# The factors of 17 norms: one power on POOL instead of twelve steps on VectorE

## The chip, the cores and the metric

The kernel runs on one core of a Trainium2 chip. The metric is device time in microseconds (us) for one execution. Engines are named as the profile names them: PE is TensorE's matmuls (PEld its weight loads), DVE is VectorE, ACT is ScalarE, POOL is GpSimd, SP is the queue that issues the plain loads and stores.

## What is computed

One layer of a decoder: 512 tokens of width 1024, three attention branches side by side, then an expert layer. Nearly every operand is normalised by its root mean square, and these norms are what the change touches:

```
def rmsnorm(x, g):                      # over 1024 columns
    y = xf * lax.rsqrt(jnp.mean(xf * xf, axis=-1, keepdims=True) + EPS)
    return (y * g).astype(x.dtype)

def head_rmsnorm(x, g):                 # over the 64 or 128 columns of a head
    return xf * lax.rsqrt(jnp.mean(xf * xf, axis=-1, keepdims=True) + EPS) * g

h = rmsnorm(x, norm1_g);  z = h @ w_in                     # queries, keys, values, gates
fq, fk, sq, sk, mq, mk = head_rmsnorm(each, its gain)      # forgetting, window, memory attention
x = x + merged @ w_out                                     # three gated branches
x = x + peer_ffn(rmsnorm(x, norm2_g), ...)                 # 8 heads, 16 of 16384 experts each
```

So a norm needs, per token (and head), one factor: (mean square + 1e-6) to the power -0.5.

## The kernel before

The 512 tokens are four blocks of 128, one token per partition. Block 0 goes first and alone through the attention branches (`mixers(0)`), the three others follow together (`mixers(1)`). Beside `mixers(1)` runs the expert work of block 0: a search for its best keys, then a long chain of gathered expert rows. For each of its 128 chosen experts POOL issues an indirect DMA of 128 rows (L828, tile `row`, five buffers), and VectorE multiplies and sums them (L838, tile `scr`, for the first table; L844, tile `mg`, for the second). After the mixers comes the search for the other three blocks on VectorE (L681 to L685), then the dense part, in which blocks 2 and 3 run against all experts as matmuls while block 1's rows are gathered; that lasts from about 858 us to the end.

Matrix products are made from three matmuls on a weight split in two parts: ScalarE rounds the raw weight into `whi` (L107), and VectorE, for some weights POOL, subtracts it from the raw one into `wlo` (L119, L117). Up to the search, a scheduler puts the instructions of each engine in an order of its own by modelled times; from the dense part on the order is that of the code. Each engine works its queue strictly in that order.

A norm has three parts. The sums of squares come from ScalarE and a sum on VectorE (`rss` for whole rows, `hss` for heads). Then `rsqrt_mean` makes the factors, at most 24 columns in one call: L183 forms `rsv` = mean + epsilon; L184 and L185 shift its bits and subtract them from a constant, which is a first guess for the result (`rsy`); L187 to L189, three times, are Newton steps through `rsa`. All twelve run on VectorE. Then the factors are used: for a whole row as a scaled identity `dg` (L209, ScalarE) with which TensorE transposes and scales at once (L222); for heads as a scaling of `qn`, on VectorE for blocks 0 and memory (L324), on ScalarE for three blocks together (L328, one instruction for each head and block), after which TensorE transposes them (L342). `rstd` (L853, L935) keeps the factors of the second norm.

There are 17 such calls, with 1 to 24 columns and 138 in all; 13 come before about 300 us, four beside the gathers or at the search (342, 431, 535 and 703 us).

Of the kernel before, what the change touches and what calls it, by code (L numbers as in the profile page):

```python
# [7 lines left out]
F32 = mybir.dt.float32  # L8
F32R = mybir.dt.float32r
BF16 = mybir.dt.bfloat16  # L10
I32 = mybir.dt.int32
U32 = mybir.dt.uint32
AF = mybir.ActivationFunctionType
OP = mybir.AluOpType
# [34 lines left out]
def tile_block(ctx: ExitStack, tc: tile.TileContext, t: dict, out: bass.AP):  # L49
    nc = tc.nc  # L50
    V, A, PE, G = nc.vector, nc.scalar, nc.tensor, nc.gpsimd

    consts = ctx.enter_context(tc.tile_pool(name="consts", bufs=1))
    big = ctx.enter_context(tc.tile_pool(name="big", bufs=1))
    small = ctx.enter_context(tc.tile_pool(name="small", bufs=4))
# [112 lines left out]

    eps = consts.tile([128, 24], F32, name="eps")
    V.memset(eps, EPS)  # L170
    magic = consts.tile([128, 24], F32, name="magic")
    V.memset(magic, float(0x5F3759DF))
    ones_i = consts.tile([128, 24], I32, name="ones_i")
    V.memset(ones_i, 1)

    def rsqrt_mean(ss, n, size):

        v = small.tile([128, 24], F32, tag="rsv", name="rsv")
        sh = small.tile([128, 24], I32, tag="rsi", name="rsi", bufs=2)
        y = small.tile([128, 24], F32, tag="rsy", name="rsy")  # L180
        a = small.tile([128, 24], F32, tag="rsa", name="rsa")
        v, sh, y, a, n = v[:, :n], sh[:, :n], y[:, :n], a[:, :n], slice(0, n)
        V.scalar_tensor_tensor(v, ss, 1.0 / size, eps[:, n], op0=OP.mult, op1=OP.add)  # L183
        V.tensor_tensor(sh, v.bitcast(I32), ones_i[:, n], op=OP.logical_shift_right)  # L184
        V.scalar_tensor_tensor(y.bitcast(I32), sh, -1.0, magic[:, n], op0=OP.mult, op1=OP.add)  # L185
        for _ in range(3):
            V.tensor_mul(a, y, y)  # L187
            V.scalar_tensor_tensor(a, a, -0.5, v, op0=OP.mult, op1=OP.mult)
            V.scalar_tensor_tensor(y, a, 1.5, y, op0=OP.add, op1=OP.mult)  # L189
        return y  # L190

    def squares(x, dst):
# [7 lines left out]
    def factors(sums, nb):  # L200

        ss = small_f(BIG, "rss", 2)[:, :nb]
        V.reduce_sum(ss, sums[:, :nb], axis=AX.X)
        return rsqrt_mean(ss, nb, D)
# [88 lines left out]
    class Heads:  # L293
# [25 lines left out]
        def scale(self):  # L319
            r = rsqrt_mean(self.ss[:, :self.cols], self.cols, self.parts[0][3])  # L320
            for z, c, nh, hd in self.parts:
                for b in range(self.nb):
                    if self.nb < BIG:
                        V.tensor_mul(z[:, b, :, :hd], z[:, b, :, :hd],  # L324
                                     r[:, c + b * nh:c + b * nh + nh, None].to_broadcast([128, nh, hd]))
                        continue
                    for h in range(nh):
                        A.activation(z[:, b, h, :hd], z[:, b, h, :hd], AF.Copy,  # L328
                                     scale=r[:, c + b * nh + h:c + b * nh + h + 1])
# [857 lines left out]
```

## Time and profile before

| | us |
|---|---|
| median of 3 runs | 1792.46 (1791.27 to 1794.70) |
| the profiled execution | 1789.02 |
| its span, first to last instruction | 1786.5 |
| busy: PE / PEld | 1646.6 / 1367.5 |
| busy: DVE | 1349.1 |
| busy: ACT | 629.5 |
| busy: POOL | 812.9 |
| mean granted TensorE clock, share of full speed | 0.954 |

The busy time of an engine is a sum over stages with different limits, so a stage is read by itself. In a row of the timeline the bracket at the end tells how long that engine had been idle and what ended the idle time. PE's busy time includes overlap of one matmul with the next.

### The profile page before, as it was taken

How to read it: one execution, taken by the hardware profiler on the slowest of the kernel's cores; microseconds unless marked ns; L12 is line 12 of the kernel's file. 1: busy time of each engine (PE TensorE's matmuls, PEld its weight loads, DVE VectorE, ACT ScalarE, POOL GpSimd, SP SyncE). 2: the span in 40 equal slices, each digit the busy share in tenths (PEclk: the TensorE clock that was granted, in tenths of full speed). 3: DMA queues.
4: the chain of work that ended last, by engine and by line, in shares of the span. 5: the costliest groups of instructions: out<-in, count | busy, mean ns of one | idle time of the engine just before them, and what ended most of it. 6: DMA issues, size and time to landing. Idle time of an engine off the chain costs nothing.

```text
span 1786.5 us, 24816 instructions
## 1 busy us (share of the span) xinstructions
PE 1646.6 (92%) x8590; PEld 1367.5 (77%) x8590; DVE 1349.1 (76%) x2717; ACT 629.5 (35%) x1416; POOL 812.9 (45%) x719
## 2 busy tenths in 40 slices
PE   6899788999999989888899979989898999999998
PEld 5898777898987989877789967767666676666664
DVE  5787647969996999999989955656566676676765
ACT  5786545564544434221136631111111111111111
POOL 1000353646553558884068853434444444444542
PEclk8998989999996999989999999999999999999998
DMA  6786455969995899785389997989899999999996
GB/s 248 224 266 188 149 146 167 329 246 327 354 322 175 313 320 330 244 276 176 142 302 401 415 398 278 387 315 391 316 384 348 368 386 376 368 381 375 391 352 217
DMA packets 216813, 540.13 MB, mean 302 GB/s; under 512 B 17008, under 2 KB 95088, under 8 KB 216688
## 3 DMA queue, kind: packets, MB, share of 16 engines
q1 hardware_dynamic: 142960, 270.09, 43.0%
q0 software_dynamic: 73728, 268.47, 41.2%
q8 instruction: 67, 1.10, 0.2%
q14 instruction: 58, 0.48, 0.1%
HBM read 519.61 MB, written 18.87 MB: 301 GB/s over the span
## 4 chain that ended last, share of the span: by engine, by line
issue 33%; DVE 13%; DMA 13%; PE 12%; POOL 12%; ACT 1%; POOLq 0%; DVEq 0%; ACTq 0%
POOL row L828 11%; DMA row<-in_peer_v_dram,eidx 7%; DMA row<-in_peer_u_dram,eidx 6%; PE mm L918 5%; DVE mg L844 4%; DVE scr L838 1%; PE mm L132 1%; PE mm L133 1%; PE mm L131 1%; DVE tmp L683 1%; PE sc L989 1%; PE tp L989 1%; DVE wlo L119 1%; PE sc L496 1%; DVE ids L682 1%
## 5 line engine op out<-in xcount | busy, mean ns | idle before, releaser
L828 POOL DMA_INDIRECT row<-in_peer_u_dram,eidx x256 | 316.7, 1237 | 387.6 <-DVE scr L838 274.8
L918 PE MATMUL mm<-h2f,two 128*128 128x256 f32 x1920 | 442.8, 382 | 16.0 <-DMA two<-in_uT_dram 10.9
L828 POOL DMA_INDIRECT row<-in_peer_v_dram,eidx x256 | 312.0, 1219 | 282.9 <-DVE mg L844 207.9
L918 PEld LDWEIGHTS mm<-h2f,two 128*128 128x128 f32 x1920 | 363.4, 192 | 82.0 <-issue 27.8
L119 DVE TENSOR_TENSOR wlo<-raw,whi 128x1024 fp32r<-128x1024 f32 (+1 forms) x201 | 245.4, 1223 | 212.9 <-ACT whi L107 209.3
L844 DVE SCALAR_TENSOR_TENSOR mg<-row,acts,mg 128x1024 f32<-128x1024 f32 x256 | 356.4, 1392 | 24.2 <-DMA row<-in_peer_v_dram,eidx 21.6
L107 ACT CAST whi<-raw 128x1024 fp32r<-128x1024 f32 (+1 forms) x236 | 246.8, 1048 | 308.7 <-DMA raw<-in_peer_v_dram 182.4
L838 DVE SCALAR_TENSOR_TENSOR scr<-row,h2n 128x1024 bf16<-128x1024 f32 x256 | 313.3, 1224 | 35.1 <-DMA row<-in_peer_u_dram,eidx 30.1
L117 POOL TENSOR_TENSOR wlo<-raw,whi 128x1024 fp32r<-128x1024 f32 (+1 forms) x35 | 83.8, 2401 | 216.8 <-ACT whi L107 216.6
L922 ACT ACTIVATE ga<-mm 128x256 f32<-128x256 f32 x128 | 49.3, 386 | 374.1 <-PE mm L918 367.4
L131 PE MATMUL mm<-whi,hhi 128*128 128x256 f32 (+1 forms) x576 | 169.0, 295 | 5.3 <-ACT hhi L633 1.9
L132 PE MATMUL mm<-wlo,hhi 128*128 128x256 f32 (+1 forms) x576 | 166.6, 290 | 2.0 <-DVE wlo L119 2.0
L133 PE MATMUL mm<-whi,hlo 128*128 128x256 f32 (+1 forms) x576 | 166.0, 290 | 2.3 <-DVE hlo L634 1.1
L1030 PE MATMUL sc<-raw,ah 128*128 128x512 f32 x256 | 121.0, 595 | 0.8 <-DVE ah L1012 0.8
L1030 PE MATMUL tp<-raw,ah 128*128 128x512 f32 x256 | 120.3, 592 | 0.0
L131 PEld LDWEIGHTS mm<-whi,hhi 128*128 128x128 f32 x576 | 111.2, 194 | 8.5 <-ACT hhi L633 2.2
L132 PEld LDWEIGHTS mm<-wlo,hhi 128*128 128x128 f32 x576 | 111.3, 193 | 5.2 <-DVE wlo L119 2.9
L133 PEld LDWEIGHTS mm<-whi,hlo 128*128 128x128 f32 x576 | 111.2, 194 | 4.4 <-DVE hlo L634 1.4
L133 PE MATMUL mm<-hhi,wlo 128*128 128x384 f32 x320 | 110.8, 346 | 3.7 <-POOL wlo L117 3.7
L131 PE MATMUL mm<-hhi,whi 128*128 128x384 f32 x320 | 111.1, 347 | 1.5 <-ACT hhi L223 1.1
L132 PE MATMUL mm<-hlo,whi 128*128 128x384 f32 x320 | 112.1, 350 | 0.0
L1030 PEld LDWEIGHTS tp<-raw,ah 128*128 128x128 f32 x256 | 48.6, 190 | 61.2 <-issue 61.2
(265 smaller groups left out, 2834.6 us busy)
## 6 DMA issues: line engine op xcount, KB each, us to landing
raw<-in_peer_v_dram SPq DMA_DIRECT2D x128, 512.0 KB
two<-in_uT_dram SPq DMA_DIRECT2D x60, 1024.0 KB
raw<-in_w_nat_dram SPq DMA_DIRECT2D x40, 512.0 KB
gd<-st SPq DMA_DIRECT2D x32, 512.0 KB
gq<-gd SPq DMA_DIRECT2D x32, 512.0 KB
raw<-in_w_tr_dram SPq DMA_DIRECT2D x48, 256.0 KB
raw<-in_w_o_dram SPq DMA_DIRECT2D x24, 512.0 KB
raw<-in_w_tr_dram SPq DMA_DIRECT2D x24, 512.0 KB
```

The lines of the kernel that those rows point to most:

```text
L107: A.copy(hi[:, :n * w], raw[:, :n * w])
L117: G.tensor_tensor(lo, raw, hi.bitcast(F32), op=OP.subtract)
L119: V.tensor_sub(lo, raw, hi.bitcast(F32))
L131: PE.matmul(ps, lh, rh, start=first, stop=False)
L132: PE.matmul(ps, lh, rl, start=False, stop=False)
L133: PE.matmul(ps, ll, rh, start=False, stop=last)
L828: G.indirect_dma_start(out=r, out_offset=None, in_=t["peer_" + tab], in_offset=bass.IndirectOffsetOnAxis(ap=eidx[b][:, j:j + 1], axis=0))
L838: V.scalar_tensor_tensor(scr, r, 1.0, h2n[b], op0=OP.mult, op1=OP.mult, accum_out=acts[b][:, c]))
L844: V.scalar_tensor_tensor(x1[b], r, acts[b][:, c], x1[b], op0=OP.mult, op1=OP.add))
L918: PE.matmul(ps[:, :TD], w[:, dc], h2f[dc], start=dc == 0, stop=dc == KC - 1)
L922: A.activation(ga[k], ps[:, :TD], AF.Gelu)
L1030: PE.matmul(acc[i, hf], al[:, tok], w[0][:, d], start=k == 0, stop=k == NK - 1)
```

## The change

`rsqrt_mean` keeps its first step on VectorE (mean plus epsilon) and gets the factors by one two-input instruction on POOL, a power with a tile of -0.5 as exponent. The shift, the subtraction and the nine Newton steps go, with their constants and two work tiles. Nothing else in the code differs; the scheduler orders all instructions anew.

```
--- before.py
+++ after.py
@@ -168,25 +168,15 @@
 
     eps = consts.tile([128, 24], F32, name="eps")
     V.memset(eps, EPS)
-    magic = consts.tile([128, 24], F32, name="magic")
-    V.memset(magic, float(0x5F3759DF))
-    ones_i = consts.tile([128, 24], I32, name="ones_i")
-    V.memset(ones_i, 1)
+    mhalf = consts.tile([128, 24], F32, name="mhalf")
+    V.memset(mhalf, -0.5)
 
     def rsqrt_mean(ss, n, size):
 
-        v = small.tile([128, 24], F32, tag="rsv", name="rsv")
-        sh = small.tile([128, 24], I32, tag="rsi", name="rsi", bufs=2)
-        y = small.tile([128, 24], F32, tag="rsy", name="rsy")
-        a = small.tile([128, 24], F32, tag="rsa", name="rsa")
-        v, sh, y, a, n = v[:, :n], sh[:, :n], y[:, :n], a[:, :n], slice(0, n)
-        V.scalar_tensor_tensor(v, ss, 1.0 / size, eps[:, n], op0=OP.mult, op1=OP.add)
-        V.tensor_tensor(sh, v.bitcast(I32), ones_i[:, n], op=OP.logical_shift_right)
-        V.scalar_tensor_tensor(y.bitcast(I32), sh, -1.0, magic[:, n], op0=OP.mult, op1=OP.add)
-        for _ in range(3):
-            V.tensor_mul(a, y, y)
-            V.scalar_tensor_tensor(a, a, -0.5, v, op0=OP.mult, op1=OP.mult)
-            V.scalar_tensor_tensor(y, a, 1.5, y, op0=OP.add, op1=OP.mult)
+        v = small.tile([128, 24], F32, tag="rsv", name="rsv")[:, :n]
+        y = small.tile([128, 24], F32, tag="rsy", name="rsy")[:, :n]
+        V.scalar_tensor_tensor(v, ss, 1.0 / size, eps[:, :n], op0=OP.mult, op1=OP.add)
+        G.tensor_tensor(y, v, mhalf[:, :n], op=OP.pow)
         return y
 
     def squares(x, dst):
```

Three places show how the order moves. The first is ScalarE's queue at the start: the first norm's `dg` (L209, in the changed code L199) and the casts `whi` of the first weights. Before:

```order
L246 ACTIVATE gcol<-gcol 128x1
L209 ACTIVATE dg<-cst,rsy 128x128
L107 CAST whi<-raw 128x1056
L223 ACTIVATE hhi<-tp,gcol 128x128
L107 CAST whi<-raw 128x1056
L223 ACTIVATE hhi<-sc,gcol 128x128
L223 ACTIVATE hhi<-tp,gcol 128x128
L223 ACTIVATE hhi<-sc,gcol 128x128
```

In the changed kernel:

```order
L236 ACTIVATE gcol<-gcol 128x1
L107 CAST whi<-raw 128x1056 x2
L199 ACTIVATE dg<-cst,rsy 128x128
L185 ACTIVATE junk,sums<-mg_247 128x1024
L213 ACTIVATE hhi<-tp,gcol 128x128
L213 ACTIVATE hhi<-sc,gcol 128x128
L185 ACTIVATE junk,sums<-mg_247 128x1024
L213 ACTIVATE hhi<-tp,gcol 128x128
```

`dg` now stands behind both casts instead of ahead of them.

The second is VectorE's queue at the norm of the first forgetting-attention heads (66 us in the trace), eight factors for queries and keys. Before, from the last sum of squares:

```order
L310 TENSOR_REDUCE hss<-sq 128x4
L119 TENSOR_TENSOR wlo<-raw,whi 128x1024
L183 SCALAR_TENSOR_TENSOR rsv<-hss,eps 128x8
L119 TENSOR_TENSOR wlo<-raw,whi 128x1024
L184 TENSOR_TENSOR rsi<-rsv,ones_i 128x8
L185 SCALAR_TENSOR_TENSOR rsy<-rsi,magic 128x8
L119 TENSOR_TENSOR wlo<-raw,whi 128x1024
L187 TENSOR_TENSOR rsa<-rsy 128x8
L119 TENSOR_TENSOR wlo<-raw,whi 128x1024
L188 SCALAR_TENSOR_TENSOR rsa<-rsa,rsv 128x8
L119 TENSOR_TENSOR wlo<-raw,whi 128x1024
L189 SCALAR_TENSOR_TENSOR rsy<-rsa,rsy 128x8
```

In the changed kernel (L178 is the step that was L183, and L314 the scaling of `qn` that was L324):

```order
L119 TENSOR_TENSOR wlo<-raw,whi 128x1024 x2
L300 TENSOR_REDUCE hss<-sq 128x4
L119 TENSOR_TENSOR wlo<-raw,whi 128x1024
L178 SCALAR_TENSOR_TENSOR rsv<-hss,eps 128x8
L119 TENSOR_TENSOR wlo<-raw,whi 128x1024 x2
L314 TENSOR_TENSOR qn<-qn,rsy 128x4x64 x2
L119 TENSOR_TENSOR wlo<-raw,whi 128x1024 x2
```

The eleven steps and the weight splits between them are gone from between the first step and the scaling; two splits are left there.

The third is POOL's queue at the gathers for block 0 (`eidx` holds the chosen experts). Before:

```order
L696 TENSOR_TENSOR cand<-v_3471 128x16
L828 DMA row<-in_peer_u_dram,eidx_187 128x1024 x128
L828 DMA row<-in_peer_v_dram,eidx_187 128x1024 x32
L117 TENSOR_TENSOR wlo<-raw,whi 128x1024
L828 DMA row<-in_peer_v_dram,eidx_187 128x1024 x4
```

In the changed kernel (L179 is the power, L818 the gather):

```order
L686 TENSOR_TENSOR cand<-v_3325 128x16
L179 TENSOR_TENSOR rsy<-rsv,mhalf 128x24
L818 DMA row<-in_peer_u_dram,eidx_173 128x1024 x16
L179 TENSOR_TENSOR rsy<-rsv,mhalf 128x24
L818 DMA row<-in_peer_u_dram,eidx_173 128x1024 x35
L179 TENSOR_TENSOR rsy<-rsv,mhalf 128x24
L818 DMA row<-in_peer_u_dram,eidx_173 128x1024 x56
L179 TENSOR_TENSOR rsy<-rsv,mhalf 128x12
L818 DMA row<-in_peer_u_dram,eidx_173 128x1024 x21
L818 DMA row<-in_peer_v_dram,eidx_173 128x1024 x35
L117 TENSOR_TENSOR wlo<-raw,whi 128x1024
```

Four powers now stand in this queue ahead of and between the gathers; one more stands further on, behind 42 gathers of the second table.

## Rows read from the trace of the kernel before

**Rows 1.** Busy us by stage: length, PE, PEld, DVE, ACT, POOL, clock, DMA share, GB/s
```profile
0.00:290.00 290.00, 245.87 (x1785) 232.09 (x1785) 194.41 (x591) 185.47 (x377) 55.42 (x63) 0.92 0.65 202
...
290.00:700.00 410.00, 388.26 (x2464) 354.86 (x2465) 355.10 (x640) 194.16 (x464) 216.49 (x168) 0.93 0.84 294
...
700.00:858.00 158.00, 134.92 (x706) 125.12 (x704) 155.07 (x630) 37.40 (x71) 108.08 (x149) 0.94 0.69 227
```

**Rows 2.** Groups by line, the removed steps: count, busy us, mean ns, idle us
```profile
L189 DVE SCALAR_TENSOR_TENSOR rsy<-rsa,rsy 128x4 f32<-128x4 f32 (+7 forms) x51 | 13.2, 266 | 0.7
...
L187 DVE TENSOR_TENSOR rsa<-rsy 128x4 f32<-128x4 f32 (+7 forms) x51 | 10.3, 209 | 0.7
...
L188 DVE SCALAR_TENSOR_TENSOR rsa<-rsa,rsv 128x4 f32<-128x4 f32 (+7 forms) x51 | 7.8, 161 | 0.6
...
L185 DVE SCALAR_TENSOR_TENSOR rsy<-rsi,magic 128x4 int32<-128x4 int32 (+7 forms) x17 | 4.7, 287 | 0.2
...
L184 DVE TENSOR_TENSOR rsi<-rsv,ones_i 128x4 int32<-128x4 int32 (+7 forms) x17 | 4.7, 286 | 0.2
```

**Rows 3.** The timeline, norms at 296 and 431 us: start, us, engine, line
```profile
295.67 0.17 DVE L183 SCALAR_TENSOR_TENSOR rsv<-hss,eps 128x24 f32<-128x24 f32 x1
...
306.25 0.18 DVE L189 SCALAR_TENSOR_TENSOR rsy<-rsa,rsy 128x24 f32<-128x24 f32 x1
...
306.46 3.69 ACT L328 ACTIVATE qn<-qn,rsy 128x64 f32<-128x64 f32 x15 [7.38 <-DVE rsy L189]
...
306.87 0.42 PE L342 MATMUL tg<-cst,qn 128*66 128x128 f32 x1 [3.44 <-ACT qn L328]
...
312.82 0.85 PE L342 MATMUL tg<-cst,qn 128*66 128x128 f32 x3 [2.90 <-ACT kT L343]
...
430.70 0.18 DVE L183 SCALAR_TENSOR_TENSOR rsv<-hss,eps 128x24 f32<-128x24 f32 x1
...
451.17 0.17 DVE L189 SCALAR_TENSOR_TENSOR rsy<-rsa,rsy 128x24 f32<-128x24 f32 x1
```

**Rows 4.** The groups by line and shape on POOL, whole span
```profile
L828 POOL DMA_INDIRECT row<-in_peer_u_dram,eidx x256 | 316.7, 1237 | 387.6 <-DVE scr L838 274.8 <-issue 39.8 <-ACT qn L328 23.1
...
L117 POOL TENSOR_TENSOR wlo<-raw,whi 128x1024 fp32r<-128x1024 f32 x34 | 81.3, 2400 | 216.8 <-ACT whi L107 216.6
...
L696 POOL TENSOR_TENSOR cand<-v 128x24 f32<-128x24 f32 x32 | 9.3, 306 | 12.5 <-DVE tmp L683 6.5 <-DVE v L681 3.7 <-DVE best L681 2.2
```

**Rows 5.** The timeline of the first three norms
```profile
4.79 4.72 POOL L265 TENSOR_SCALAR slope<-cst 128x128 bf16<-128x128 f32 x8 [4.35 <-DMA cst<-in_c_mats_dram]
...
8.60 0.40 ACT L209 ACTIVATE dg<-cst,rsy 128x128 f32<-128x128 f32 x1 [2.32 <-DVE rsy L189]
...
10.70 1.07 ACT L107 CAST whi<-raw 128x1056 fp32r<-128x1056 f32 x1 [0.45 <-DMA raw<-in_w_skvf_dram]
...
24.04 0.48 PE L342 MATMUL tg<-cst,qn 128*128 128x128 f32 x1 [5.47 <-DVE qn L324]
```

**Rows 6.** The timeline of the norms at 66 and 243 us
```profile
66.17 0.16 DVE L183 SCALAR_TENSOR_TENSOR rsv<-hss,eps 128x8 f32<-128x8 f32 x1
...
75.17 0.17 DVE L189 SCALAR_TENSOR_TENSOR rsy<-rsa,rsy 128x8 f32<-128x8 f32 x1
...
75.95 0.60 PE L342 MATMUL tg<-cst,qn 128*66 128x128 f32 x4 [3.83 <-DVE qn L324]
...
251.45 1.43 PE L342 MATMUL tg<-cst,qn 128*128 128x128 f32 x3 [3.09 <-ACT qn L328]
```

**Rows 7.** The timeline of the last norm
```profile
707.81 2.96 DVE L189 SCALAR_TENSOR_TENSOR rsy<-rsa,rsy 128x3 f32<-128x3 f32 x1
...
708.33 2.41 POOL L117 TENSOR_TENSOR wlo<-raw,whi 128x1024 fp32r<-128x1024 f32 x1
...
718.27 2.62 DVE L189 SCALAR_TENSOR_TENSOR rsy<-rsa,rsy 128x3 f32<-128x3 f32 x1
...
722.85 2.08 PE L222 MATMUL tp<-dg,mg 128*128 128x128 f32 x8 [5.00 <-ACT dg L209]
```

## The prediction

> **What bounds the kernel now.** I read the busy times by stage first, then the steps of the 17 norms (one call of `rsqrt_mean` each), then what TensorE and ScalarE waited for right behind a norm, and last the POOL queue, where the new instruction will stand.
>
> The stage table [rows 1] has three stretches that hold norms. From 0 to 290 us (the first token block, alone) TensorE is busy 245.9 of 290 us and VectorE 194.4, so neither is full: time goes to waits of one on the other. From 290 to 700 us (the other three blocks beside the gathered expert rows) TensorE is busy 388.3 of 410 us and VectorE 355.1. From 700 to 858 us (the search for the best keys) VectorE is busy 155.1 of 158 us and sets the pace. After 858 us there is no norm, and the code there is the same before and after, so what the norms give or cost early I carry to the end one for one.
>
> The norms' own steps are cheap in busy time [rows 2]: the 187 steps that go (17 shifts, 17 subtractions, three times 17 of each Newton line) hold VectorE for 4.7 + 4.7 + 10.3 + 7.8 + 13.2 = 40.7 us, 2.3% of the span. What counts more is how long a factor takes. The steps depend on one another and the queue mixes other work between them, so the 24 factors of one norm take from 295.67 to 306.43 us, 10.8 us for twelve instructions of 0.18 us; ScalarE sits idle 7.38 us for them, and TensorE 3.44 us and then 2.90 us [rows 3]. Another norm of 24 takes from 430.70 to 451.34 us, 20.6 us [rows 3]. So the question is how long one power takes from start to result, against 4 to 21 us for the chain it replaces.
>
> **What is added: one power on POOL.** The trace of before holds no power. The nearest row below is an addition on POOL with the same shape, 128x24: 306 ns [rows 4]. The nearest above is the largest two-input operation on POOL, 128x1024, with 2,400 ns for 43 times as many columns [rows 4]. A power needs more arithmetic per element than an addition, but it is unlikely to need 43 times as much, so I take 1 us for 24 columns, nearer to the row of its own shape, and keep 0.3 and 2.4 us as ends. A gain on VectorE below nothing is excluded only if the result comes sooner than now, which both ends allow. With about 0.2 us for each of two hand-overs the result comes 1.4 us after the first step, against 10.8 us.
>
> Where it stands: in the changed order the powers of the gather stage stand between gathers. Waiting for a power's input holds the gathers queued behind it, and for those VectorE's products wait. But POOL spends 274.8 us waiting for exactly these products [rows 4], each power stands five gathers behind the product ahead of its first step (16 gathers against 11 products, 51 against 46, 107 against 102, with five row buffers), so POOL gets there when VectorE does. I cost this queue at nothing; without that cover it costs one gather, 1.24 us [rows 4], for each of four powers.
>
> **What is removed, norm by norm.** The first norm gets worse: eight scalings hold POOL from 4.79 to 9.51 us [rows 5] and stand ahead of the power, and ScalarE now has both weight casts ahead of the scaled identity `dg`. The second cast starts at 10.70 us, when its weights have landed, and takes 1.07 us [rows 5], so `dg` moves from 8.60 to about 11.8 us. The two casts (2.1 us) no longer stand behind it, which leaves about 1.1 us lost. The second and third norms, one queue step instead of eleven, take some 2 of the 5.47 us that TensorE waits at 24.04 us [rows 5]. Net gain 1 us, ends -1.1 and 3.
>
> The norm at 66 us takes 9.2 us (66.17 to 75.34) with VectorE's weight splits between its steps, and TensorE waits 3.83 us for it [rows 6]. In the changed order two splits of 1.2 us stand between first step and use, and the power hides behind them: gain 3.8 us, ends 0 and 3.8. The norm at 243 us leaves TensorE waiting 3.09 us [rows 6]: gain 3.1 us, ends 0 and 3.1. The norm at 296 us is the largest: ScalarE could start its 24 scalings about 7 us sooner, and TensorE's two waits sum to 6.3 us [rows 3]. The scalings still take 6 us and the transposes now mix with matmuls, so I take 5 us, ends 0 and 6.3.
>
> The next three norms (342, 431 and 535 us) have no such TensorE wait; they free 3 x 11 x 0.18 = 5.9 us of VectorE in a stage where it is busy 355 of 410 us. I take 2 us, ends 0 and 5.9. The last norm lies in the search stage, where VectorE is the bound: 11 steps of 0.15 us are 1.7 us. Two of its steps took 2.96 and 2.62 us because they were held, the first while a weight split ran on POOL from 708.33 to 710.74 us [rows 7]; such a hold moves to the next two-input step, so I count it at nothing and keep 6 us as the upper end. TensorE's 5.00 us at 722.85 [rows 7] shrink too, but VectorE is what is late next there.
>
> Sum: 1 + 3.8 + 3.1 + 5 + 2 + 1.7 = 16.6 us, less about 0.4 us at six places where something now waits for the power and its hand-overs, 2.5 us: a gain of 14 us. All upper ends together are 28 us; with the long power (2.4 us) another 8 us go, which leaves 6. The profiled execution took 1789.0 us, its span 1786.5; the median of the runs is 3.4 us above that execution. 14 us off the profiled one is 1775, off the median 1778.5 us, which is what I forecast.
>
> **A rule against it.** The held step [rows 7] shows that a two-input operation on POOL shuts out one on VectorE: it ended at 710.77 us, 0.03 us after the split on POOL. The Trainium skill (Perfetto Trace Analysis, Optimizing Scalar/DVE Operations) says that the two engines share a read port, so that moving work between them might not help. The trace agrees on the hold. By that rule the power, itself with two inputs, would give back on VectorE what it frees there, and the sum would be that of the first rival.
>
> **Rivals.** (1) The gain is given back. Each power keeps two-input work off VectorE while it runs, and VectorE now meets the consumer of the factor two or three places behind the first step, so it idles where it used to work. With 138 columns in all 17 norms, at some 0.2 us a column (5 us for 24) powers hold POOL for 28 us; shut-out and waits then cost about the 14 us, and the time is 1792 us. For it: the hold above. Against it: the price is twice my upper end. (2) Slower: the power is a long loop. From 0.45 us a column (10.8 us for 24) it takes longer than the chain it replaces at 296 us. At 1 us a column the four norms from 296 to 535 us take 24, 24, 24 and 12 us, VectorE gets nothing done with two inputs meanwhile, and gathers stand behind it: against 10.8 and 20.6 us [rows 3] that is 13 and 3 us longer, with the two norms between and after them and the narrow ones about 30 us in all, so 1822 us. Against it: no POOL row comes near such a price per column. (3) The waits that go are hidden anyway. TensorE's idle time behind a norm is filled by the next wait (the weights, the casts), the new order loses its 1.1 us at the start, and only VectorE's 1.7 us in the search are left: 1791 us.
>
> **How the numbers follow.** The forecast has 0.64, rival 1 has 0.13, rival 2 0.13 and rival 3 0.10. A difference of 0.2% (3.6 us) is about what a measurement of this kernel tells from no change. The forecast's cases are nearly all faster, a few of them by less than that; rivals 1 and 3 are mostly within it, with some of rival 1 on either side. So: faster 0.65, same 0.18, slower 0.17. The range runs from all upper ends, 1764 us, to a little beyond no gain, 1797 us, which leaves out most of rival 2 and the best and worst mixes.
>
> **What would show it.** Right: the powers on POOL take near 1 us for 24 columns; the TensorE waits of 3.83, 3.09 and 3.44 us behind the scaled queries and keys are gone or below 1 us; ScalarE's 7.38 us at 306 us are below 2 us; `dg` of the first norm starts near 11.8 us; the search stage is about 2 us shorter; and from the first matmul of the dense stage to the end the span keeps its length. Wrong: powers of 5 us or more, VectorE idle in front of its multiplications by the factor, gathers idle behind a power, or a dense stage of another length, which would mean that the early time is not carried to the end.

## The result and the profile after

| | before | after |
|---|---|---|
| median of the runs of one chip, us | 1788.78 (1773.23 to 1794.70, 6 runs) | 1775.71 (1768.19 to 1776.39, 6 runs) |
| the profiled execution, us | 1789.02 | 1776.12 |
| its span, us | 1786.5 | 1773.6 |
| PE / DVE / POOL busy, us | 1646.6 / 1349.1 / 812.9 | 1628.8 / 1312.1 / 844.2 |

The ratio of the times is 0.9928 with a 95% interval of 0.9899 to 0.9957: the changed kernel is faster by 0.4 to 1.0%, some 13 us. The forecast was 14 us.

The stages of the changed kernel answer to [rows 1]; columns as there. From 290 to 700 us POOL is busy 33.6 us more and TensorE 5.9 us less.

```profile
0.00:290.00 290.00, 250.89 (x1887) 237.79 (x1887) 187.72 (x482) 188.83 (x384) 76.36 (x76) 0.95 0.68 210
290.00:700.00 410.00, 382.40 (x2437) 350.38 (x2438) 355.06 (x596) 195.91 (x466) 250.09 (x183) 0.95 0.86 302
700.00:858.00 158.00, 137.75 (x721) 127.37 (x721) 149.93 (x659) 36.27 (x69) 86.50 (x139) 0.95 0.65 216
```

The power itself: first its group on the page of the changed kernel, with busy time and mean ns ahead of the second bar's idle time, then the answer for its line, with shortest, median and longest duration in ns and who waited for it.

```profile
L179 POOL TENSOR_TENSOR rsy<-rsv,mhalf 128x4 f32<-128x4 f32 (+7 forms) x17 | 37.5, 2210 | 130.3 <-DVE rsv L178 130.1
```

```profile
L179 POOL TENSOR_TENSOR rsy<-rsv,mhalf x17: 557/1232/9467, 9.5 to 689.8; 128x4 f32<-128x4 f32 x3, 128x8 f32<-128x8 f32 x3, 128x24 f32<-128x24 f32 x3, 128x1 f32<-128x1 f32 x2
...
who waited for it (us, times):
  ACT qn L318: 8.2, 3
  DVE rstd L925: 1.7, 1
  ACT dg L199: 1.7, 1
  DVE rstd L843: 0.7, 1
  DVE qn L314: 0.5, 1
```

ScalarE's scalings of `qn` waited 8.2 us for powers, and 6.32 us of that belong to one norm, as the timeline shows (start us, duration, engine, line; the bracket is the idle time before and what ended it). The answers to [rows 5], [rows 6], [rows 3] and [rows 7], in that order:

```profile
9.51 0.58 POOL L179 TENSOR_TENSOR rsy<-rsv,mhalf 128x1 f32<-128x1 f32 x1
12.09 0.40 ACT L199 ACTIVATE dg<-cst,rsy 128x128 f32<-128x128 f32 x1
12.54 0.80 PE L212 MATMUL tp<-dg,mg 128*128 128x128 f32 x2 [12.54 <-ACT dg L199]
22.88 0.33 PE L332 MATMUL tg<-cst,qn 128*128 128x128 f32 x1 [3.10 <-DVE qn L314]
51.82 1.01 POOL L179 TENSOR_TENSOR rsy<-rsv,mhalf 128x4 f32<-128x4 f32 x1 [9.70 <-DVE rsv L178]
64.88 0.16 DVE L178 SCALAR_TENSOR_TENSOR rsv<-hss,eps 128x8 f32<-128x8 f32 x1
65.18 2.49 POOL L179 TENSOR_TENSOR rsy<-rsv,mhalf 128x8 f32<-128x8 f32 x1 [12.35 <-DVE rsv L178]
69.37 0.60 PE L332 MATMUL tg<-cst,qn 128*66 128x128 f32 x4
74.52 1.64 POOL L179 TENSOR_TENSOR rsy<-rsv,mhalf 128x8 f32<-128x8 f32 x1 [6.85 <-DVE rsv L178]
240.13 0.81 PE L332 MATMUL tg<-cst,qn 128*128 128x128 f32 x2 [1.21 <-ACT qn L318]
282.85 9.47 POOL L179 TENSOR_TENSOR rsy<-rsv,mhalf 128x24 f32<-128x24 f32 x1 [11.10 <-DVE rsv L178]
282.89 1.22 DVE L786 TENSOR_TENSOR hot<-hot,idb 128x2048 bf16<-128x2048 bf16 x1
289.90 1.23 DVE L786 TENSOR_TENSOR hot<-hot,idb 128x2048 bf16<-128x2048 bf16 x1
292.35 5.83 ACT L318 ACTIVATE qn<-qn,rsy 128x64 f32<-128x64 f32 x24 [6.32 <-POOL rsy L179]
292.75 0.30 PE L332 MATMUL tg<-cst,qn 128*66 128x128 f32 x1 [3.03 <-ACT qn L318]
298.70 0.85 PE L332 MATMUL tg<-cst,qn 128*66 128x128 f32 x3 [2.91 <-ACT kT L333]
326.16 5.18 POOL L179 TENSOR_TENSOR rsy<-rsv,mhalf 128x24 f32<-128x24 f32 x1
414.32 4.78 POOL L179 TENSOR_TENSOR rsy<-rsv,mhalf 128x24 f32<-128x24 f32 x1
691.34 1.16 PE L212 MATMUL tp<-dg,mg 128*128 128x128 f32 x8 [1.23 <-ACT dg L199]
```

The wait of 3.83 us behind the norm at 66 us is gone, 3.09 became 1.21, the last norm's 5.00 became 1.23. At the first 24-column norm, now at 283 us, little moved: ScalarE waited 7.38 us before and 6.32 now, TensorE 3.44 and 2.90 before and 3.03 and 2.91 now. The reason stands in the same rows: that power took 9.47 us. That its end is where the profile puts it is seen from ScalarE, which starts 0.03 us after it. The Trainium skill (Perfetto Trace Analysis, GPSIMD Engine Instruction) advises to distrust spans on this engine and to go by the distance of starts; here the two agree, within 0.1 us, as two powers in a row show below.

To see where the time went I take the lead of the changed kernel at points that both traces have, on the start of the same instruction:

| point | before, us | after, us | lead |
|---|---|---|---|
| first matmul | 9.05 | 12.54 | -3.5 |
| 200th matmul | 48.64 | 47.34 | 1.3 |
| norm at 80 us, first step | 80.13 | 74.18 | 6.0 |
| norm at 243 us, first step | 243.16 | 236.18 | 7.0 |
| norm at 296 us, first step | 295.67 | 282.59 | 13.1 |
| 2000th matmul, behind that norm | 328.22 | 313.43 | 14.8 |
| last norm, first step | 702.53 | 686.54 | 16.0 |
| first sum of the dense part, `o` (L971, then L961) | 916.19 | 894.37 | 21.8 |
| end | 1786.51 | 1773.61 | 12.9 |

What this lead is made of shows in TensorE, which runs the same 5195 matmuls ahead of that first sum in both kernels. Columns as in [rows 1]; before, before once more (from the first experiment below), after, after once more:

```profile
0.00:916.20 916.20, 824.43 (x5195) 759.80 (x5195) 755.11 (x1961) 425.28 (x930) 391.48 (x389) 0.93 0.74 248
0.00:913.20 913.20, 818.42 (x5195) 755.47 (x5195) 755.76 (x1960) 424.85 (x930) 392.69 (x389) 0.94 0.73 249
0.00:894.40 894.40, 804.04 (x5195) 744.05 (x5195) 718.16 (x1773) 425.33 (x930) 423.67 (x406) 0.95 0.76 256
0.00:898.20 898.20, 808.09 (x5195) 747.76 (x5195) 718.23 (x1772) 424.61 (x930) 421.82 (x406) 0.94 0.75 255
```

TensorE's idle time, the length less its busy time, is 91.8 us before and 90.4 after (94.8 and 90.1 in the repeated pair). Its busy time on the same matmuls is 20.4 us shorter (10.3). So most of the lead is not idle time that went: the same matmuls ran at a higher granted clock. In the trace's clock rows TensorE stood at the lower of its two levels (0.50 of full speed, 1.2 GHz) for 126 us of this stretch before and for 82 after (116 and 99). An engine that is kept busy loses half of such time, so the 44 us (17) less are worth some 22 us (9), an estimate, about what the busy time shrank by. The longest such stretch lies behind the norm at 535 us, before and then after:

```profile
534.40:568.50 34.10, 32.36 (x111) 23.87 (x111) 20.92 (x61) 14.98 (x46) 10.31 (x9) 0.50 0.50 168
536.20:546.40 10.20, 8.25 (x30) 6.33 (x31) 4.94 (x13) 6.78 (x20) 6.07 (x5) 0.50 0.87 308
```

Before once more it is 23.9 us long, so part of the difference changes from run to run. Another begins as TensorE's wait of 3.09 us ends (251.45 us): from 251.1 to 264.7 us the clock stands at 0.50. In the changed kernel that wait is 1.21 us, ends at 240.13, and the clock stands at 0.50 for 3.4 us from 246.1 on.

22 us ahead at the dense part's first sum, 13 us ahead at the end: the dense stage, which holds no norm, became 9 us longer. Its busy times from that sum to the end, before and then after:

```profile
916.20:1786.50 870.30, 822.17 (x3395) 607.73 (x3395) 594.00 (x757) 204.24 (x486) 421.38 (x330) 0.98 0.96 359
```

```profile
894.40:1773.60 879.20, 824.79 (x3395) 610.26 (x3395) 593.95 (x757) 203.80 (x486) 420.50 (x330) 0.97 0.95 354
```

The work is the same (3395 matmuls, VectorE busy 594.0 us in both), and the DMA engines move the same loads at 354 instead of 359 GB/s. So two questions go to the experiments: what makes the early part shorter, and what makes the dense stage longer.

### The profile page after: what moved, and what is told of

Same layout as the page of the kernel before. It is cut to its first block, busy times and chain, and to the rows that moved or that the text cites. A ratio compares the mean times of both kernels' runs of the same rounds, so it can differ in the third digit from the quotient of the medians.

```text
span 1773.6 us, 24656 instructions
## 1 busy us (share of the span) xinstructions
PE 1628.8 (92%) x8590; PEld 1354.3 (76%) x8590; DVE 1312.1 (74%) x2529; ACT 629.1 (35%) x1416; POOL 844.2 (48%) x736
## 4 chain that ended last, share of the span: by engine, by line
issue 34%; PE 26%; DMA 13%; POOL 13%; DVE 10%; ACT 3%; SPq 0%; POOLq 0%; DVEq 0%; ACTq 0%
POOL row L818 11%; DMA row<-in_peer_v_dram,eidx 6%; PE mm L908 6%; DMA row<-in_peer_u_dram,eidx 5%; PE mm L131 4%; PE mm L132 4%; PE mm L133 4%; DVE mg L834 3%; DMA two<-in_uT_dram 1%; POOL rsy L179 1%; DVE wlo L119 1%; PE sc L979 1%; PE tp L979 1%; DVE tmp L673 1%; PE sc L486 1%
## 5 line engine op out<-in xcount | busy, mean ns | idle before, releaser
L818 POOL DMA_INDIRECT row<-in_peer_u_dram,eidx x256 | 315.2, 1231 | 359.0 <-DVE scr L828 288.8
L818 POOL DMA_INDIRECT row<-in_peer_v_dram,eidx x256 | 314.8, 1230 | 284.9 <-DVE mg L834 215.3
L834 DVE SCALAR_TENSOR_TENSOR mg<-row,acts,mg 128x1024 f32<-128x1024 f32 x256 | 349.2, 1364 | 25.4 <-DMA row<-in_peer_v_dram,eidx 22.4
L828 DVE SCALAR_TENSOR_TENSOR scr<-row,h2n 128x1024 bf16<-128x1024 f32 x256 | 313.7, 1225 | 27.1 <-DMA row<-in_peer_u_dram,eidx 19.4
L179 POOL TENSOR_TENSOR rsy<-rsv,mhalf 128x4 f32<-128x4 f32 (+7 forms) x17 | 37.5, 2210 | 130.3 <-DVE rsv L178 130.1
```

Source lines behind the costliest of these rows:

```text
L179: G.tensor_tensor(y, v, mhalf[:, :n], op=OP.pow)
L818: G.indirect_dma_start(out=r, out_offset=None, in_=t["peer_" + tab], in_offset=bass.IndirectOffsetOnAxis(ap=eidx[b][:, j:j + 1], axis=0))
L828: V.scalar_tensor_tensor(scr, r, 1.0, h2n[b], op0=OP.mult, op1=OP.mult, accum_out=acts[b][:, c]))
L834: V.scalar_tensor_tensor(x1[b], r, acts[b][:, c], x1[b], op0=OP.mult, op1=OP.add))
```

## The experiments

In the code cuts `...` stands for lines left out, `..` for `mybir.EngineType.`; constants such as `mhalf` and `one` (tiles of -0.5 and 1) are made as in the change. In each experiment the profiled execution gives the first `o` and the dense stage's length (end of the span less first `o`), and the timed runs a ratio to the kernel before, run on the same chip between them.

### The same two kernels again

Both kernels unchanged, to learn how well the points repeat.

> The kernel before, once more, for a second trace. In the first pair of traces the changed kernel is 21.8 us ahead when VectorE writes the first tile `o` of the dense stage (894.4 against 916.2 us) but only 12.9 us ahead at the end: the dense stage is 879.2 us long instead of 870.3. If that is the stage's own spread from run to run, the stage of before is away from 870 us by 5 to 10 us here. If it comes from the new order of the loads and of ScalarE, it is 870 us within 2.

> The changed kernel once more. The first `o` should come at 894 us within 2. If the dense stage's length is spread, it is away from 879 us by 5 to 10 us; if the order sets it, it is 879 us within 2, and the kernel stays about 9 us short of its early lead.

Measured: before again, first `o` at 913.2 us, dense stage 865.9 us, ratio 1.0023 [0.9993, 1.0053]; after again, 898.2 and 878.6 us, 1774.78 us, ratio 0.9934 [0.9909, 0.9960]. The result holds. The points repeat less well than expected: the first `o` of the changed kernel came 4 us later, the dense stage of the kernel before is 4 us shorter, and both were expected within 2. The lead at the first `o` is 15 to 22 us, depending on which two of these four traces are compared; the dense stage is 12.7 us longer in this pair, 8.9 in the first.

### The removed steps stay on VectorE, their result unused

```
         V.scalar_tensor_tensor(v, ss, 1.0 / size, eps[:, n], op0=OP.mult, op1=OP.add)
+        p = small.tile([128, 24], F32, tag="rsp", name="rsp")[:, n]
+        G.tensor_tensor(p, v, mhalf[:, n], op=OP.pow)
...
-        return y
+        return p
```

> The factors come from the power, and VectorE also does the eleven removed steps, whose result nobody uses. Theory chain (the gain is the shorter time from the sums to the factors): the first `o` is 15 to 20 us earlier than before, the total 0.5 to 0.9% faster than before. Theory load (the gain is 187 fewer instructions on VectorE): 0 to 5 us earlier, total within 0.3% of before.

Measured: first `o` at 894.3 us, dense stage 881.5 us, 1773.48 us, ratio 0.9942 [0.9915, 0.9970], against 0.9934 for the changed kernel. The removed steps are back (their groups hold VectorE for 45.3 us here, 40.7 in [rows 2]), and nothing is lost. The gain comes from the length of the chain that a factor goes through, not VectorE's load.

This trace has a second use. Its first 24-column power (`rsp` here) was short, and ScalarE's wait with it:

```profile
281.77 5.32 POOL L187 TENSOR_TENSOR rsp<-rsv,mhalf 128x24 f32<-128x24 f32 x1 [11.09 <-DVE rsv L185]
...
287.12 5.84 ACT L332 ACTIVATE qn<-qn,rsp 128x64 f32<-128x64 f32 x24 [2.15 <-POOL rsp L187]
```

From the last matmul ahead of this norm to the 2000th the lead grew by 6.8 us here (14.2 to 21.0) and by 1.7 us in the changed kernel. So the 5 us that the prediction gave this norm are there when the power takes 5 us, and are not when it takes 9.5; some 2 us of the difference are the clock's, with 3.4 us at the lower level from the 1750th to the 2000th matmul here and 10.2 in the changed kernel. They did not last: at the first `o` the two kernels are 21.9 and 21.8 us ahead.

### No root at all

The power is left out, and mean plus epsilon stands as the factor: the root is not computed, everything else is.

```
-        G.tensor_tensor(y, v, mhalf[:, :n], op=OP.pow)
+        y = v
```

> No power and no Newton step: the first step's result, mean plus epsilon, stands in for the factor, so the root is left out of the computation. It has VectorE's load of the changed kernel and no wait for POOL. Theory chain: the powers that held up ScalarE and TensorE (the first norm, the one at 283 us with 9.5 us, those of 24 columns) cost 5 to 12 us of the lead, so the first `o` comes 27 to 34 us earlier than before. Theory load: 20 to 24 us earlier, as in the changed kernel.

Measured: first `o` at 877.1 us, dense stage 868.4 us, 1754.47 us, ratio 0.9843 [0.9810, 0.9875]. A factor that costs nothing brings 39 us up to the first `o`, more than the 27 to 34 expected; the powers get 18 to 22 of them and cost the rest. And the dense stage is as long as before, though it is reached 39 us earlier.

### The power for narrow norms alone, and for wide ones alone

```
+        if n.stop <= 8:
+            G.tensor_tensor(y, v, mhalf[:, n], op=OP.pow)
+            return y
```

Thirteen norms of 1 to 8 columns take the power, the four of 12 and 24 columns keep the steps; the second kernel has `> 8`.

> The power for the 13 norms of up to 8 columns, the Newton steps on VectorE for the four of 12 and 24 columns (283 to 534 us). Theory chain: the lead of the first 283 us stays (13 us) and the wide norms, where a power takes 4.8 to 9.5 us, lose little or win: first `o` 15 to 22 us earlier than before. Theory load: 13 of 17 norms, so 76% of 22 us, 17 us. If the power of the wide norms costs more than it saves, this kernel is ahead of the changed one.

> The other half: the power for the four norms of 12 and 24 columns, the Newton steps for the 13 others. Theory chain: at 283 us nothing is gained, from there to the first `o` 5 to 9 us. Theory load: 4 of 17 norms, 24% of 22 us, 5 us. If the two halves do not add up to 22 us, the order that the scheduler makes anew for every kernel has a share of that size.

Measured: narrow alone, first `o` at 884.1 us (32 us ahead), dense stage 880.0 us, 1772.71 us, ratio 0.9938 [0.9912, 0.9963]; wide alone, 919.7 us (3.5 us behind), 871.9 us, ratio 1.0025 [1.0002, 1.0048]. The early gain comes from the narrow norms. On the 24 columns the power wins nothing at the first norm and 10 us go somewhere behind it: between the narrow kernel and the changed one the leads differ by 2 us ahead of the first wide norm (15.1 and 13.1 us) and by 10 at the first `o`. Both leads miss what was expected (15 to 22 us and 5 to 9 us), and the halves add up to 28.5 us instead of 21.8: by what was written ahead, the order that is made anew for each kernel has a share of some 7 us. Nor does the narrow kernel's lead all reach the end: its dense stage is long too.

### Two powers in a row

The mean goes to the power 1 first, then to -0.5, so that each factor costs two powers.

```
-        G.tensor_tensor(y, v, mhalf[:, :n], op=OP.pow)
+        z = small.tile([128, 24], F32, tag="rsz", name="rsz")[:, :n]
+        G.tensor_tensor(z, v, one[:, :n], op=OP.pow)
+        G.tensor_tensor(y, z, mhalf[:, :n], op=OP.pow)
```

> Each norm takes two powers in a row on POOL, the first with exponent 1, which leaves the value as it is; the result is the same. One more power costs 0.56 us (1 column) to 4.8 us (24 columns) and 28 us over all 17. Theory chain: most of it shows, the first `o` comes 10 to 20 us later than in the changed kernel. Theory load: VectorE's load is as in the changed kernel, so at most 4 us later, from the shared port.

Measured: first `o` at 906.2 us (10 us ahead), dense stage 878.8 us, 1789.01 us, ratio 1.0023 [0.9998, 1.0047]. Doubling the price of the power takes back the whole gain, about 14 us against the changed kernel's 1774.78. The pair at the first wide norm:

```profile
285.34 9.47 POOL L182 TENSOR_TENSOR rsz<-rsv,one 128x24 f32<-128x24 f32 x1 [11.10 <-DVE rsv L180]
294.89 4.27 POOL L183 TENSOR_TENSOR rsy<-rsz,mhalf 128x24 f32<-128x24 f32 x1
```

Start to start they are 9.55 us apart, so the long span is real. The first runs beside VectorE's expert selection (`hot`, up to 1.23 us a piece, two inputs), the second behind most of it. The same 24 columns cost 4.3 us in one place and 9.5 in the other.

### The dense part's loads in the order of the code

From here on the question is the dense stage. Ahead of the prediction I wrote that from the dense part on the order is that of the code. That is true of TensorE, VectorE and POOL alone; ScalarE and SP are still put in order by the scheduler, and a new start gives them a new order. These three kernels (before, after and the narrow one) put SP in code order as well.

```
-    ctx.enter_context(tc.manual_schedule(engines={..Pool, ..DVE, ..PE}))
+    ctx.enter_context(tc.manual_schedule(engines={..Pool, ..DVE, ..PE, ..SP}))
```

> The kernel before, with the loads on SP, from the dense part on, in the order of the code instead of the scheduler's. It is the partner for the next two kernels, which have the same order of loads there. First `o` at 915 us within 3, as before. How long the dense stage is in this order is open; what counts is that the next two show the same length.

> The changed kernel with the loads of the dense part in the order of the code. Theory order (the scheduler, given other modelled times early on, puts the loads of the dense part in another order, and that order makes the stage 9 to 11 us longer): first `o` 18 to 22 us ahead of the partner, dense stage as long as the partner's within 3 us, end 16 to 22 us ahead. Theory arrival (the stage takes longer because it begins earlier, whatever the order): dense stage 8 to 11 us longer than the partner's, end 9 to 13 us ahead.

> Power for the 13 norms of up to 8 columns, Newton steps for the four wide ones, loads of the dense part in the order of the code. Theory order: first `o` about 30 us ahead of the partner, the same dense stage within 3 us, end 27 to 33 us ahead, and faster than the changed kernel by 0.5% or more if the order of the code is no worse than the scheduler's. Theory arrival: end 17 to 22 us ahead.

Measured: first `o` at 935.8, 919.1 and 916.7 us; dense stages 1018.7, 1021.7 and 1027.5 us; medians 1962.29, 1942.57 and 1942.56 us. The stage is 150 us longer with the same work and the code's order of loads, its DMA engines 84% busy instead of 95 to 97%, and the first `o` comes 20 us later than the 915 us expected; that is a poor base for telling 9 us apart. By the medians nearly 20 us reach the end, all of the lead at the first `o` (17 and 19 us), which speaks for the order. By the single traces it is 14 and 10, and the narrow kernel's stage is 9 us longer than its partner's on the same order of loads, which speaks for the rival. The runs show how much hangs on the order of loads; they don't settle whose order cost the 9 us.

### Two kernels that differ in one narrow norm

The last pair keeps the steps in the four wide norms and in one narrow one: the second norm in the first kernel, the first norm in the other.

```
+        calls[0] += 1
+        if calls[0] in [1, 3, 4, 5, 6, 7, 8, 9, 10, 11, 12, 17]:     # the other: [2, 3, 4, ...]
+            G.tensor_tensor(y, v, mhalf[:, n], op=OP.pow)
+            return y
```

They were chosen by what the scheduler makes of them: the first issues its dense part's 247 loads and stores in just the order of the kernel before (on ScalarE 2 of 488 instructions moved), the other within one row in the order of the changed kernel, which is 8 moved rows from before (and 32 on ScalarE). Rows count as moved that have to be taken out and put elsewhere to get one order of names from the other.

> The power stands in twelve of the thirteen narrow norms (up to 8 columns); the second norm and the four wide ones keep the guess and the steps. The loads of the dense stage are issued in the same order as in the kernel before. Theory that the order of loads made the changed kernel's dense stage longer: first expert sum (first o) 27 to 32 us earlier than before (916.2 us), the stage from there to the end 866 to 871 us as before, the end 27 to 32 us earlier, about 1755 to 1760 us as median, faster than both kernels. Rival, that a dense stage that is reached early simply waits longer for its weights: the same first o, the stage 878 to 886 us, the end 18 to 22 us earlier, about 1766 to 1771 us.

> As the other kernel of this call, but the first norm keeps the guess and the steps and the second has the power. The loads of the dense stage are issued in the changed kernel's order, within one row. Theory of the order: first o 27 to 32 us earlier than before, the stage from there to the end 877 to 882 us, the end 15 to 22 us earlier, about 10 us behind the other kernel of this call. Rival, that an early arrival waits for weights: the stage and the median within 3 us of the other kernel's.

Measured: with before's order, first `o` at 897.4 us, dense stage 868.9 us, 1769.35 us, ratio 0.9908 [0.9880, 0.9935]; with the changed kernel's order, 892.6 us, 886.7 us, 1782.69 us, ratio 0.9995 [0.9972, 1.0019]. The kernel that reaches the dense part 5 us later ends 13 us earlier. The leads at the first `o` (18.8 and 23.6 us) fell short of the 27 to 32 us that both theories expected: undoing the power in one narrow norm costs more early time than I thought. On the dense stage the theory of the order is borne out in sign, with 18 us instead of some 10 (877 to 882 us were expected of the second), and the rival, within 3 us of each other, falls. Half of the 18 us is idle time of TensorE, 45.5 and 54.6 us; the other half is busy time on the same 3395 matmuls (823.3 and 832.1 us), with 35 and 61 us at the lower clock.

All eleven dense stages with the scheduler's order, by how many of the 247 loads and stores moved against before:

| kernel | first `o`, us | moved | dense stage, us |
|---|---|---|---|
| no root | 877.1 | 0 | 868.4 |
| power in 12 norms, not the second | 897.4 | 0 | 868.9 |
| before, twice | 916.2, 913.2 | 0 | 870.3, 865.9 |
| wide alone | 919.7 | 1 | 871.9 |
| narrow alone | 884.1 | 3 | 880.0 |
| two powers | 906.2 | 3 | 878.8 |
| after, twice | 894.4, 898.2 | 8 | 879.2, 878.6 |
| steps kept unused | 894.3 | 8 | 881.5 |
| power in 12 norms, not the first | 892.6 | 9 | 886.7 |

At most one row moved: 866 to 872 us; three or more: 879 to 887 us, and when the stage is reached makes no difference in either group. ScalarE's order is made anew in the same step and was not varied alone.

The same eleven traces tell whether the clock of the early part is chance. Ahead of the first `o` TensorE stood at its lower level for 113 to 126 us in the three with the steps in the narrow norms (before, twice, and wide alone) and for 68 to 99 us in the eight with the power or nothing there, so it goes with the change. It does not order the leads by itself: two powers and no root have 68 us each and are 29 us apart, with 104.9 and 77.4 us of idle time on TensorE. No run varied the clock alone.

One of the three moved rows of the narrow kernel can be followed in its trace. The scheduler's order there, before (and in the kernel without the second norm's power) on the left, narrow on the right; `two` is 1 MB of expert keys, `raw` 0.5 MB of expert values:

```
gq<-gd               gq<-gd
gq<-gd               gq<-gd
raw<-in_peer_v       two<-in_uT
two<-in_uT           raw<-in_peer_v
raw<-in_peer_v       raw<-in_peer_v
```

First SP, ScalarE, VectorE and TensorE of the narrow kernel, then the same place in the kernel with before's order:

```profile
1498.04 1.24 SPq L1011 DMA_DIRECT2D gq<-gd  x2
1501.22 4.78 SPq L918 DMA_DIRECT2D two<-in_uT_dram  x1
1506.11 0.88 SPq L100 DMA_DIRECT2D raw<-in_peer_v_dram  x2
...
1521.39 1.04 ACT L107 CAST whi<-raw 128x1024 fp32r<-128x1024 f32 x1 [12.88 <-DMA raw<-in_peer_v_dram]
...
1522.46 1.23 DVE L119 TENSOR_TENSOR wlo<-raw,whi 128x1024 fp32r<-128x1024 f32 x1 [11.01 <-ACT whi L107]
...
1524.57 0.79 PE L131 MATMUL sc<-whi,ah 128*128 128x512 f32 x1 [6.84 <-ACT ah L126]
```

```profile
1507.68 1.24 SPq L1013 DMA_DIRECT2D gq<-gd  x2
1511.48 1.54 SPq L100 DMA_DIRECT2D raw<-in_peer_v_dram  x1
1513.12 0.39 SPq L920 DMA_DIRECT2D two<-in_uT_dram  x1
...
1524.83 1.04 ACT L107 CAST whi<-raw 128x1024 fp32r<-128x1024 f32 x1 [6.67 <-DMA raw<-in_peer_v_dram]
...
1525.91 1.23 DVE L119 TENSOR_TENSOR wlo<-raw,whi 128x1024 fp32r<-128x1024 f32 x1 [5.72 <-ACT whi L107]
```

In the narrow kernel `two` sits at the head of the queue for 4.78 us, since it waits for TensorE (`tp`, by the waits of this queue), and `raw` stands behind it: from the `gq` pair to the first `raw` it is 8.07 us instead of 3.80. ScalarE then waits 12.88 us for a `raw` instead of 6.67, VectorE, whose queue is in code order, 11.01 instead of 5.72, and TensorE 6.84 us; with before's order TensorE has no wait of 2 us or more between 1507 and 1540 us. Around the end of this wait the granted clock stands at 0.50, from 1522.1 to 1528.9 us. Over 100 matmuls at this place (the 7700th to the 7800th) the narrow kernel takes 36.2 us, the kernel with two powers 35.4 and the one without the first norm's power 31.9, and these three have the swap; the other eight traces take 27.1 to 28.6. This one swap is most of the extra 9 to 11 us of the first two.

The changed kernel does not have it and loses elsewhere. Another `two` stands ahead of a `raw` at its 153rd row: from the 7400th to the 7500th matmul the four traces with this swap (the changed kernel twice, the steps kept unused, the power not in the first norm) take 29.9 to 35.8 us, two powers 29.0 and the six others 26.9. From the 6900th to the 7000th matmul it takes 31.6 and 31.4 us instead of 26.5, but so nearly does the wide kernel (30.4), and the kernel without the first norm's power, with the same loads there, does not (26.5): the cause of that part is open. The same wait shows in the changed kernel: TensorE's waits in its dense stage, by line, in the changed kernel and then before (total us, times, longest).

```profile
PE sc L131 <- ACT ah L126: 36.3, 13, 6.6
```

```profile
PE sc L131 <- ACT ah L126: 29.1, 13, 5.7
```

## Why the prediction was right, and where it was not

The time was right (1778.5 forecast, 1775.7 measured), and so were the sign and the lever, the latency of a factor. But three steps were wrong (what a removed wait is worth, the price of the power, the dense stage), they nearly cancel, and that the number came out so close is luck.

**What bounds the kernel, and what the change is worth.** That latency counts and not VectorE's 40.7 us held: the kernel that kept those steps unused ran as fast as the one without them. But the sum priced it in idle time alone and put the granted clock at nothing. Against the 14 us of its sum, 1.4 us of TensorE's idle time are gone at the first `o` (4.7 in the repeated pair). Idle time did go where the norms stood (6.0 to 1.0 us between the 200th and the 800th matmul), and some came back later (21.6 to 25.4 us from the 4400th matmul to the first `o`; 23.0 to 25.4). The rest of the lead, 20.4 us (10.3), is busy time, with less time at the lower clock.

**The price of the power** was the mis-sized term. I took 1 us for 24 columns and 2.4 at most, by the nearest POOL rows [rows 4]; it is 0.57 us for one column, 1.01 for four and mostly 1.64 for eight; for 24 it is 4.78, 5.18 and 9.47 us in the changed kernel and 4.27 at the least in any, that is at best about 0.4 us and 0.16 us per column. That is near the first rival's 0.2 us per column, and two of the three wide powers are above what the text named as a sign of being wrong, 5 us. The hand-overs, put at 0.2 us each, took 0.09 and 0.03 us at that norm. That the total still held has two reasons besides the clock. The narrow norms, where the price was about as assumed, carry the early gain. And the rival's consequence, VectorE idle in front of its multiplications, did not follow: of all waits for a power VectorE has 2.9 us. Doubled, the power does take the whole gain, so the forecast was nearer to that rival than its 0.13 says.

**The start.** Forecast `dg` near 11.8 us and a net gain of 1 us: `dg` starts at 12.09, the first matmul is 3.5 us late, the 200th 1.3 us early. Right.

**The norms at 66 and 243 us.** Forecast 3.8 and 3.1 us. The lead grew by 4.7 us (from 1.3 to 6.0) over the first and by 6.1 us from the first step of the second to that of the next wide norm, with the first TensorE wait gone and the second cut to 1.21. The first is right: the lead there is idle time. The second is right by half: from the 1400th to the 1750th matmul idle time falls by 2.2 us and busy time by 4.3, with 3.4 us at the lower clock instead of 14.3.

**The norm at 296 us.** Forecast 5 us, got at most 1.7 (lead 13.1 to 14.8). The step that failed is the price above: 9.47 us of power in place of a chain of 10.8 us.

**The gather stage, the last norm and the search.** Forecast 2 + 1.7 us, got 7.0 us between the 2000th matmul and the first `o` in the first pair and 0.4 in the repeated one. Between the 3000th and the 3500th matmul alone the first pair differs by 8.7 us, with 34.1 and 10.2 us at the lower clock. From the last norm's first step to the first `o` it is 5.8 and 2.6 us shorter, where 1.7 were forecast. The cover over POOL's queue held, though for another reason than the number given: the 274.8 us [rows 4] are of the whole span. From 290 to 880 us POOL waits 82.5 us for VectorE's products of the first table before and 82.8 after, and VectorE waits 15.0 and 6.8 us for its gathered rows (0.4 and 6.3 for the second table's).

**The dense stage.** "The code there is the same before and after", so the early gain was to reach the end one for one. That failed, and it is the instructive step: the code is the same but ScalarE's and SP's orders are not, and 9 to 13 of the 15 to 22 us were given back there, at the loads that were swapped as far as the traces tell. The text had named a dense stage of another length as a sign of this. It was in reach ahead of time, since the changed order of SP could be read next to the old one; I looked at the queues around the norms only.

**The sum.** Forecast 14 us early and 14 at the end. Measured 15 to 22 early and, by the medians, 10 to 13 at the end. With before's order of loads, twelve of the powers gave 1769.35 us, 0.9908 [0.9880, 0.9935]: it beats the kernel before, and the changed one by some 5 us by the ratios, though the intervals of the two ratios overlap.

## What to carry to other kernels

A dependent chain of short steps costs far more than its busy time where its queue is shared; one slow instruction elsewhere can beat it, up to the width at which its own time reaches the chain's, so price it by its widest use. When a scheduler makes the order anew, compare the orders of all queues to the end of the program, also where the code did not change: a load that was swapped with its neighbour can cost more than the edit gains. A lead that is measured at the start of a stage is a gain only if the stage behind it is as long as before. And a removed wait has to be looked for in TensorE's busy time as well as in its idle time, since the granted clock can move by more than the wait.

## What the runs showed of the hardware

A power on POOL took 0.55 to 0.58 us for one column of 128 rows in most places, 1.01 for four, 1.64 to 2.49 for eight and 4.27 to 5.32 for 24; an estimate from the shortest is 0.4 us and 0.16 us per column. At the first 24-column norm it took 9.47 to 9.50 us in the changed kernel, in the wide one and as the first of two powers. What stretches it there is not shown: VectorE's work beside it is nearly the same in the kernel that kept the steps, where it took 5.32 us.

It is not that one engine locks the other out for the whole of an instruction: the power began at 282.85 us, VectorE's `hot` 0.04 us behind it took its usual 1.22 us, and so did the next at 289.90. The Trainium skill (SBUF — State Buffer, SBUF: two separate sides) says that of such a pair whoever starts first holds the shared ports for its whole instruction and the other blocks; a hold stands in [rows 7], where VectorE's step ended 0.03 us after POOL's weight split, but for a power this trace does not agree, and the measurement decides.

The granted clock can carry a gain: with 1.4 us less idle time ahead of the first `o`, the same 5195 matmuls held TensorE for 804.0 instead of 824.4 us, with 82 instead of 126 us at the lower of its two levels.

The dense stage ran from 866 to 887 us with its DMA engines 95 to 97% busy, and 1,019 to 1,027 us with another order of loads in one queue and the DMA engines 84% busy, on the same matmuls.
